# Two chains of attention maps in the second block, and joined small operations

## The chip, the cores and the metric

The kernel runs on one core of a Trainium2 chip. The metric is device microseconds (us) of one execution; lower is better. A core has a matrix engine (PE, with its weight loads shown apart as PEld), a vector engine (DVE), a scalar engine (ACT), a general engine (POOL) and a queue engine (SP) that issues most transfers. Each engine works through its own list of instructions in order, and waits at an instruction until what that instruction needs is there.

## The reference, cut to what matters

The program is two blocks of two layers on one sequence of 256 tokens and width 1024. The change lies in the second block alone, in its mixers; a layer there is:

```python
a = rms_norm_2(h, norm_attn[i])
u = a @ w_in[i]
(nsa_q, k_cmp, v_cmp, k_slc, v_slc, k_win, v_win, nsa_g, d_q, d_k, d_v,
 g_q, g_k, g_v, g_lr, g_og, r_q, r_f, r_i, r_og) = split_cols(u, IN_SPLITS_2)
o_a = nsa_attention(...)    # NSA: selected + window attention, a compressed branch, sigmoid gates
o_b = diff_attention(...)   # softmax(q0 k0) - lambda * softmax(q1 k1), times v, then an rms norm
o_c = gla_mixer(...)        # gated linear attention
o_d = hgrn2_mixer(...)      # gated linear attention with its own gate
h = h + jnp.concatenate([o_a, o_b, o_c, o_d], axis=-1) @ w_out[i]
...                         # a dense feed-forward (layer 0) or eight experts (layer 1)
```

and of the two mixers whose maps move:

```python
q = rms_norm_2(q, qk_gain[0])                       # NSA: also of k_slc and k_win
p = jax.nn.softmax(jnp.where(m, s, NEG), axis=-1)   # per head, causal
o = g[..., 0:1] * o_c + g[..., 1:2] * o_s + g[..., 2:3] * o_w
...
w = p[:, :, 0] - lam_full * p[:, :, 1]              # differential attention
o = rms_norm_2(einsum(w, v), sub_gain) * (1.0 - lam_init)
```

## The kernel before, in words

A projection is done in single-precision pieces: a 1 MB block of weights arrives by DMA (`raw`), ACT casts its high part (`whi`, line 142), DVE or POOL subtracts to get the low part (`wlo`, line 145), and PE does three products with the activations' high and low parts (lines 151 to 153). The 256 tokens are two tiles of 128, `tt` = 0 and 1.

`block2_mixers` runs once for each layer and does, in program order: the projection of the differential queries and keys, whose evacuation `ev_dqk` (lines 1216 to 1234) squares, sums, takes a power and scales; two projections for NSA and the differential values (`nsa`, `dv`); NSA's norms (squares `nsq` on POOL, sums `nr` on DVE, the power in `powm`, line 243, on POOL, the scaling `qn` on DVE, transposes `nqt` on PE); the compressed branch (`BT`, then the products `hp`); a projection for the linear attentions' values (tiles of 272 columns); the gate of gated linear attention (`glt`, `gp`, `gy`, with a logarithm on ACT); the channel projections (`pc`); seven *levels* (lines 1622 to 1684) that build the linear attentions' triangular matrices `AT`, each with the factors `E` and `Q` on DVE, an exponential on ACT, `Kt` on POOL, products `pg` and `ph` on PE and a masked copy on DVE; the *maps*; the projections of the output gates; norms, the transposes of `mix` (`ptr`, line 281) and the output projection.

A map is one softmax attention: `nsa_a`/`nsa_b` for a pair of heads of NSA, `diff_a`/`diff_b` for a pair of the differential mixer. The first half computes scores (`nl`, `dl`) and the softmax, the second transposes (`npt`, `dpt`), multiplies with the values (`npo`, `dpo`) and writes `mix`. There are eight per layer, and before the change all stand in one staggered chain: the second half of a map follows the first half of the next. Their PSUM tiles come from a ring of three (`pst`); the projections have another ring of three (`k.pmm`).

The order on each engine isn't written out by hand. The framework places instructions by a priority (the program order, or the number in `tc.cur_priority`) against its own estimate of when they can start. A tile of a ring waits until the tile that many turns earlier is no longer read; the working tiles `n2` of 128x512 numbers are a ring of six. The maps get the priority of an earlier place in the program:

```python
first = tc.cur_priority
...
last, tc.cur_priority = tc.cur_priority, first
staggered([(kind, tt, m) for tt in range(2) for m in range(2) for kind in (1, 0)], [map_a, map_b])
tc.cur_priority = last
```

Of the kernel before, what the change touches and what calls it, by code (L numbers as in the profile page):

```python
# [10 lines left out]
F32 = mybir.dt.float32  # L11
# [1114 lines left out]
def level_tiles(k):  # L1126

    k.qbg = k.lvl.tile([P, 2, 4, P], F32, tag="qbg", name="qbg")
    k.qbh = k.lvl.tile([P, 2, 2, 2, P], F32, tag="qbh", name="qbh")
    k.AT = k.lvl.tile([P, 2, 8, P], F32, tag="AT", name="AT")  # L1130
    k.nc.gpsimd.memset(k.qbg, 0.0)
    k.nc.gpsimd.memset(k.qbh, 0.0)
# [53 lines left out]
def block2_mixers(k, a, l, hl, pre):  # L1186
# [5 lines left out]
    with ExitStack() as es:  # L1192
# [8 lines left out]

        def w2(name):
            return k.lvl.tile([P, 512], F32, tag="w2", name=name, bufs=3)
# [12 lines left out]
        def ev_dqk(tt, ps):  # L1216
            sq = n2("dsq").rearrange("p (g d) -> p g d", d=32)
            nc.scalar.activation(sq, ps.rearrange("p (g d) -> p g d", d=32), AF.Square)
# [4 lines left out]
            dqk = n2("dqk").rearrange("p (g d) -> p g d", d=32)  # L1223
            nc.vector.tensor_tensor(dqk, ps.rearrange("p (g d) -> p g d", d=32),
                                    r[:, :, None].to_broadcast([P, 16, 32]), op=ALU.mult)
# [27 lines left out]
        proj_tok(k, [w[:, 512:652], w[:, 1164:1420]], 396, hl, ev_nd)  # L1253

# [34 lines left out]
        gates = one.tile([P, 2, 12], F32, name="ngate")  # L1289
        nc.scalar.activation(gates, nsa[:, :, 640:652], AF.Tanh, scale=0.5)  # L1290
        nc.vector.tensor_scalar(gates, gates, 0.5, 0.5, op0=ALU.mult, op1=ALU.add)
        g3 = gates.rearrange("p t (h g) -> p t h g", g=3)

# [116 lines left out]
        def softmax_map(lp, S, n, sc, name):  # L1410

            mx = sm.tile([P, n], F32, tag="mx", name="mx", bufs=8)
            nc.vector.tensor_reduce(mx, lp, axis=AX.X, op=ALU.max)
            nc.vector.tensor_scalar(mx, mx, -sc, None, op0=ALU.mult)
            su = sm.tile([P, n], F32, tag="su", name="su", bufs=12)
            pr = n2(name).rearrange("p (n s) -> p n s", n=n)
            for j in range(n):
                nc.scalar.activation(pr[:, j, :S], lp[:, j, :], AF.Exp, scale=sc, bias=mx[:, j : j + 1],
                                     accum_out=su[:, j : j + 1])
            return pr, su  # L1420

        def transposed(pr, tt, name):
            pt = pst(name).rearrange("p (n s t) -> p n s t", n=2, s=2)
            for n in range(2):
                for st in range(tt + 1):
                    nc.tensor.transpose(pt[:, n, st, :], pr[:, n, st * P : (st + 1) * P], k.ident)
            prT = n2(name + "T").rearrange("p (n s t) -> p n s t", n=2, s=2)
            nc.scalar.copy(prT[:, :, : tt + 1], pt[:, :, : tt + 1])
            return prT


        def nsa_a(kind, tt, m):
            S = P * (tt + 1)
            sl = slice(tt * P, (tt + 1) * P)
            lps = [pst(f"nl{j}").rearrange("p (n s) -> p n s", n=2) for j in range(2)]
            for n, kT in enumerate((kTs, kTw)):
                for j in range(2):
                    rows = slice(64 * j, 64 * j + 64)
                    nc.tensor.matmul(lps[j][:, n, :S], qT[rows, m, sl], kT[rows, :S], start=True, stop=False)
                for j in range(2):  # L1440
                    nc.tensor.matmul(lps[j][:, n, S - P : S], k.identb, k.ntrib, start=False, stop=True)
            r = []
            for j in range(2):
                pr, su = softmax_map(lps[j][:, :, :S], S, 2, 0.125, "npr")
                nc.vector.reciprocal(su, su)
                nc.vector.tensor_tensor(su, su, g3[:, tt, 2 * m + j, 1:3], op=ALU.mult)
                r.append((pr, su))
            return r

        def nsa_b(r, kind, tt, m):  # L1450
            for j in range(2):
                h = 2 * m + j
                pr, su = r[j]
                prT = transposed(pr, tt, "npt")
                po = pst("npo")[:, :128].rearrange("p (n d) -> p n d", n=2)
                for n in range(2):
                    vo = (448, 576)[n]
                    for st in range(tt + 1):
                        nc.tensor.matmul(po[:, n, :], prT[:, n, st, :], nsa[:, st, vo : vo + 64],
                                         start=st == 0, stop=st == tt)  # L1460
                o = mix[:, tt, O_NSA + 64 * h : O_NSA + 64 * h + 64]
                for n in range(2):
                    nc.vector.scalar_tensor_tensor(o, po[:, n, :], su[:, n : n + 1], o, op0=ALU.mult, op1=ALU.add)

        dsc = 32**-0.5

        def diff_a(kind, tt, par):

            S = P * (tt + 1)
            sl = slice(tt * P, (tt + 1) * P)  # L1470
            lps = [pst(f"dl{cc}").rearrange("p (n s) -> p n s", n=2) for cc in range(2)]
            for n in range(2):
                for cc in range(2):
                    rows = slice(32 * (2 * par + cc), 32 * (2 * par + cc) + 32)
                    nc.tensor.matmul(lps[cc][:, n, :S], dT[rows, n, sl], dT[rows, 2 + n, :S], start=True, stop=False)
                for cc in range(2):
                    nc.tensor.matmul(lps[cc][:, n, S - P : S], k.identb, k.ntrib, start=False, stop=True)
            e0, s0 = softmax_map(lps[0][:, :, :S], S, 2, dsc, "de0")
            e1, s1 = softmax_map(lps[1][:, :, :S], S, 2, dsc, "de1")
            nc.vector.reciprocal(s1, s1)  # L1480
            nc.vector.scalar_tensor_tensor(s1, s1, r2.nlam, s0, op0=ALU.mult, op1=ALU.mult)
            nc.vector.reciprocal(s0, s0)
            for n in range(2):
                nc.vector.scalar_tensor_tensor(e0[:, n, :S], e1[:, n, :S], s1[:, n : n + 1], e0[:, n, :S],
                                               op0=ALU.mult, op1=ALU.add)
            return e0, s0

        def diff_b(r, kind, tt, par):
            e0, s0 = r
            prT = transposed(e0, tt, "dpt")  # L1490
            po = pst("dpo")[:, :128].rearrange("p (n d) -> p n d", n=2)
            for n in range(2):
                h = 2 * n + par
                for st in range(tt + 1):
                    nc.tensor.matmul(po[:, n, :], prT[:, n, st, :], dv[:, st, 64 * h : 64 * h + 64],
                                     start=st == 0, stop=st == tt)
            for n in range(2):
                h = 2 * n + par
                nc.vector.tensor_scalar(mix[:, tt, O_DIFF + 64 * h : O_DIFF + 64 * h + 64], po[:, n, :],
                                        s0[:, n : n + 1], None, op0=ALU.mult)  # L1500
            if par == 1:

                mv = mix[:, tt, O_DIFF : O_DIFF + 256].rearrange("p (g d) -> p g d", d=64)
                sq = n2("dsq")[:, :256].rearrange("p (g d) -> p g d", d=64)
                nc.gpsimd.tensor_tensor(sq, mv, mv, op=ALU.mult)
                ss = sm.tile([P, 4], F32, tag="dss", name="dss")
                nc.vector.tensor_reduce(ss, sq, axis=AX.X, op=ALU.add)
                nc.vector.tensor_scalar(ss, ss, 1.0 / 64, EPS, op0=ALU.mult, op1=ALU.add)
                powm(k, ss, ss, -0.5)
                for g in range(4):  # L1510
                    o = mv[:, g]
                    nc.vector.scalar_tensor_tensor(o, o, ss[:, g : g + 1], r2.on[:, 0, :], op0=ALU.mult, op1=ALU.mult)

# [84 lines left out]
        for tt in range(2):  # L1598
            nc.gpsimd.tensor_tensor(k.AT[:, tt], k.ident[:, None].to_broadcast([P, 8, P]),
                                dg[:, tt, :, None].to_broadcast([P, 8, P]), op=ALU.mult)  # L1600
# [15 lines left out]
        for i, s in enumerate(LEVELS):  # L1616
# [27 lines left out]
            for tt in range(2):  # L1644
# [3 lines left out]
                for cb in range(2):  # L1648
                    nc.tensor.matmul(ph[:, tt, 2 * cb : 2 * cb + 2], Kt[:, 1 + cb, sl], Qh[:, cb, :, hs],
                                     start=True, stop=True)  # L1650
            for o, ps in ((0, pg), (4, ph)):
                if s >= 32:

                    for b in range(0, P, 2 * s):
# [503 lines left out]
```

## Time and profile before

| | us |
|---|---|
| median of three runs (lowest, highest) | 2427.41 (2426.46, 2427.61) |
| the profiled execution | 2425.61 |
| its span, first to last instruction | 2423.5 |
| PE busy | 2324.4 (96%) |
| DVE busy | 1873.6 (77%) |
| ACT busy | 1491.0 (62%) |
| POOL busy | 408.9 (17%) |

The mean granted TensorE clock is 0.986 of its full rate. On the time line the mixers of the second block's layer 0 lie at about 704 to 869 us and those of layer 1 at about 1174 to 1331 us; the eight experts follow and run to the end. In the rows below a time line gives start, duration, engine, line, operation, tiles (result <- inputs), shapes, count and, in brackets, how long the engine was idle before it and which instruction ended that. A row of windows gives a stretch, its length, and the busy time of each engine in it with the number of instructions.

### The profile page before, as it was taken

To read this page: it belongs to the slowest core of one execution; us is meant where nothing else is said; L and a number is where in the kernel's file an instruction comes from. 1 tells how busy PE (TensorE), PEld (TensorE's weight loads), DVE (VectorE), ACT (ScalarE), POOL (GpSimd) and SP (SyncE) were. 2 spreads that over 40 slices of the span, in tenths; PEclk is the share of its full clock that TensorE was granted. 3 is DMA by queue.
4 is the path that set the end of the run, shared out by engine and by line. 5 is a ranking of instruction groups with operands and counts; after the bars stand their busy time and mean duration, and the time that the engine had idled before them with its cause. 6 is when DMAs were issued, how large, how long until landed. Compare 5 with 4: busy or idle time off the path is not lost. (4 is left out here: it accounts for less than half of the span.)

```text
span 2423.5 us, 35194 instructions
## 1 busy us (share of the span) xinstructions
PE 2324.4 (96%) x13123; PEld 1949.1 (80%) x13123; DVE 1873.6 (77%) x2844; ACT 1491.0 (62%) x2333; POOL 408.9 (17%) x424
## 2 busy tenths in 40 slices
PE   8999999999999799999988999999999999999997
PEld 7898879888878689998776787887878777877775
DVE  5958576776766855556577799989998989898985
ACT  5455454455545754445466677777777777776763
POOL 3534114532142321111432100000000000000000
PEclk9999999999999899999999999999999999999998
DMA  8343254343346135555540999999999999999972
GB/s 249 105 139 123 88 170 158 122 140 108 128 153 199 40 131 180 186 189 182 164 157 25 351 364 345 371 331 364 361 349 330 354 345 346 346 350 348 345 256 88
DMA packets 288735, 550.07 MB, mean 227 GB/s; under 512 B 17414, under 2 KB 95020, under 8 KB 288300
## 3 DMA queue, kind: packets, MB, share of 16 engines
q1 hardware_dynamic: 287372, 546.67, 64.4%
q8 instruction: 105, 1.72, 0.3%
q0 software_dynamic: 144, 1.05, 0.1%
q14 instruction: 74, 0.61, 0.1%
q10 hardware_dynamic: 1040, 0.03, 0.0%
HBM read 545.61 MB, written 2.10 MB: 226 GB/s over the span
## 5 line engine op out<-in xcount | busy, mean ns | idle before, releaser
L145 DVE TENSOR_TENSOR wlo<-raw,whi 128x1024 fp32r<-128x1024 f32 x948 | 1143.2, 1236 | 267.8 <-ACT whi L142 260.5
L142 ACT CAST whi<-raw 128x1024 fp32r<-128x1024 f32 x984 | 1009.0, 1048 | 436.8 <-PE pt L153 92.1
L151 PE MATMUL pt<-whi,xh 128*128 128x512 f32 (+3 forms) x656 | 251.5, 395 | 14.6 <-DVE q L612 3.0
L152 PE MATMUL pt<-wlo,xh 128*128 128x512 f32 (+3 forms) x656 | 257.3, 393 | 2.9 <-DVE wlo L145 2.6
L153 PE MATMUL pt<-whi,xl 128*128 128x512 f32 (+3 forms) x656 | 253.0, 387 | 0.0
L243 POOL TENSOR_TENSOR nr<-nms,pwm 128x1 f32<-128x1 f32 x16 | 8.7, 547 | 1135.1 <-DVE nms L258 1135.0
L152 PE MATMUL mg<-wlo,xg 128*128 128x512 f32 x448 | 180.4, 403 | 3.3 <-DVE wlo L145 3.3
L152 PE MATMUL mu<-wlo,xg 128*128 128x512 f32 x448 | 179.1, 400 | 3.1 <-DVE wlo L145 3.1
L152 PE MATMUL ya<-wlo,hh 128*128 128x512 f32 x448 | 177.5, 397 | 0.1
L151 PE MATMUL mg<-whi,xg 128*128 128x512 f32 x448 | 177.2, 396 | 0.0
L153 PE MATMUL mg<-whi,xg 128*128 128x512 f32 x448 | 177.1, 395 | 0.0
L151 PE MATMUL mu<-whi,xg 128*128 128x512 f32 x448 | 177.0, 395 | 0.0
L153 PE MATMUL mu<-whi,xg 128*128 128x512 f32 x448 | 176.9, 395 | 0.0
L153 PE MATMUL ya<-whi,hl 128*128 128x512 f32 x448 | 175.8, 393 | 0.0
L151 PEld LDWEIGHTS pt<-whi,xh 128*128 128x128 f32 x656 | 124.9, 192 | 40.9 <-issue 8.7
L151 PE MATMUL pc<-xh,whi 128*128 128x256 f32 (+1 forms) x496 | 143.9, 290 | 5.8 <-DVE q L611 2.2
L152 PEld LDWEIGHTS pt<-wlo,xh 128*128 128x128 f32 x656 | 126.0, 192 | 28.4 <-DVE wlo L145 5.5
L151 PE MATMUL ya<-whi,hh 128*128 128x512 f32 x448 | 140.6, 394 | 5.6 <-ACT whi L142 5.6
L153 PEld LDWEIGHTS pt<-whi,xl 128*128 128x128 f32 x656 | 125.2, 191 | 22.8 <-DVE xl L284 1.1
L152 PE MATMUL pc<-xl,whi 128*128 128x256 f32 (+1 forms) x496 | 142.8, 288 | 0.0
L153 PE MATMUL pc<-xh,wlo 128*128 128x256 f32 (+1 forms) x496 | 142.7, 288 | 0.0
L151 PE MATMUL gu<-xh,whi 128*128 128x256 f32 x448 | 126.7, 283 | 0.0
(643 smaller groups left out, 4718.0 us busy)
## 6 DMA issues: line engine op xcount, KB each, us to landing
raw<-in_moe_w_gate SPq DMA_DIRECT2D x112, 1024.0 KB, 6.8
raw<-in_moe_w_up SPq DMA_DIRECT2D x112, 1024.0 KB, 6.7
raw<-in_moe_w_down SPq DMA_DIRECT2D x112, 1024.0 KB, 6.7
raw<-in_w_in SPq DMA_DIRECT2D x92, 1024.0 KB, 5.1
raw<-in_w_out SPq DMA_DIRECT2D x16, 1024.0 KB, 5.0
raw<-in_ffn_w_gate SPq DMA_DIRECT2D x14, 1024.0 KB, 5.1
raw<-in_ffn_w_up SPq DMA_DIRECT2D x14, 1024.0 KB, 5.3
raw<-in_ffn_w_down SPq DMA_DIRECT2D x14, 1024.0 KB, 5.6
```

The lines of the kernel that those rows point to most:

```text
L142: nc.scalar.copy(hi, raw_view)
L145: k.last_split = eng.tensor_sub(lo, raw_view, hi)
L151: nc.tensor.matmul(out, lh, rh, start=start, stop=False)
L152: nc.tensor.matmul(out, lh, rl, start=False, stop=False)
L153: return nc.tensor.matmul(out, ll, rh, start=False, stop=stop)
L243: return k.nc.gpsimd.tensor_tensor(out, in_, k.pw[e][:, :n], op=ALU.pow)
```

## The change

Four things are edited, all in `block2_mixers`. First, `ev_dqk` copies its PSUM tile to SBUF at once (ACT), and squares and scales from the copy. Second, the maps are issued in two chains. The differential maps of tile 0 are issued right after the projections of `nsa` and `dv`, ahead of NSA's norms, and NSA's maps of tile 0 at the place of the old chain, both from the old ring; the maps of tile 1 are issued after the last gate projection, from the projections' ring. Third, small operations are joined: one scaling of the maxima, one reciprocal and one gate product for two maps, one transposed tile and copy for two NSA heads of tile 0, one `npo` tile for two heads. `AT` gets another layout, so that two masked copies become one of double size. Fourth, the differential norm's last step, four DVE instructions of 64 columns, becomes one DVE product with the row norms and one POOL product with the gain.

```diff
         def ev_dqk(tt, ps):
+            dqk = n2("dqk").rearrange("p (g d) -> p g d", d=32)
+            nc.scalar.copy(dqk, ps.rearrange("p (g d) -> p g d", d=32))
             sq = n2("dsq").rearrange("p (g d) -> p g d", d=32)
-            nc.scalar.activation(sq, ps.rearrange("p (g d) -> p g d", d=32), AF.Square)
+            nc.scalar.activation(sq, dqk, AF.Square)
...
-            dqk = n2("dqk").rearrange("p (g d) -> p g d", d=32)
-            nc.vector.tensor_tensor(dqk, ps.rearrange("p (g d) -> p g d", d=32),
-                                    r[:, :, None].to_broadcast([P, 16, 32]), op=ALU.mult)
+            nc.vector.tensor_tensor(dqk, dqk, r[:, :, None].to_broadcast([P, 16, 32]), op=ALU.mult)
...
+        def softmax_maps(lps, S, sc, names):
+            mx = sm.tile([P, 2, 2], F32, tag="mx", name="mx", bufs=4)
+            for i, lp in enumerate(lps):
+                nc.vector.tensor_reduce(mx[:, i], lp[:, :, :S], axis=AX.X, op=ALU.max)
+            nc.vector.tensor_scalar(mx, mx, -sc, None, op0=ALU.mult)
...
+            if tt:
+                prTs = [transposed([pr], tt, "npt")[0] for pr, _ in r]
+            else:
+                prTs = transposed([pr for pr, _ in r], tt, "npt")
+            po = ring[0]("npo")[:, :256].rearrange("p (j n d) -> p j n d", j=2, n=2)
...
-                for g in range(4):
-                    o = mv[:, g]
-                    nc.vector.scalar_tensor_tensor(o, o, ss[:, g : g + 1], r2.on[:, 0, :], op0=ALU.mult, op1=ALU.mult)
+                nc.vector.tensor_tensor(mv, mv, ss[:, :, None].to_broadcast([P, 4, 64]), op=ALU.mult)
+                nc.gpsimd.tensor_tensor(mv, mv, r2.on[:, 0:1, :].to_broadcast([P, 4, 64]), op=ALU.mult)
+        def run(items, r):
+            ring[0] = r
+            staggered(items, [lambda kind, *it: (nsa_a, diff_a)[kind](kind, *it),
+                              lambda r, kind, *it: (nsa_b, diff_b)[kind](r, kind, *it)])
+        beside, done = ring
+        run([(1, 0, 0), (1, 0, 1)], beside)
...
-                for tt in range(2):
-                    nc.vector.copy_predicated(od4(k.AT[:, tt, o : o + 4, :]),
-                                              bs(k.lvm[s])[:, None].to_broadcast([P, 4, 64 // s, s]),
-                                              bs4(ps[:, tt]))
+                th = lambda ap: ap.rearrange("p t h i -> p (t h) i")
+                nc.vector.copy_predicated(od4(th(k.AT[:, o])),
+                                          bs(k.lvm[s])[:, None].to_broadcast([P, 8, 64 // s, s]), bs4(th(ps)))
...
-        staggered([(kind, tt, m) for tt in range(2) for m in range(2) for kind in (1, 0)], [map_a, map_b])
-        tc.cur_priority = last
+        run([(0, 0, 0), (0, 0, 1)], beside)
+        first, tc.cur_priority = tc.cur_priority, last
...
         proj_tok(k, w[:, 2716:3228], 512, hl, ev_rio)
+        last, tc.cur_priority = tc.cur_priority, first
+        run([(1, 1, 0), (0, 1, 0), (1, 1, 1), (0, 1, 1)], done)
+        tc.cur_priority = last
```

Two places of the resulting order matter. The first is POOL in layer 0, from the last product `dqk` of the differential keys to the clearing of the compressed branch's tiles `BT`. In the kernel before it is

```order
L145 TENSOR_TENSOR wlo<-raw,whi 128x792
L1228 TENSOR_TENSOR dqk<-dqk,bc_dqk_7484 128x256 x2
L1261 TENSOR_TENSOR nsq<-nsa 128x256
L1262 TENSOR_TENSOR nsq<-nsa 128x64
...
L145 TENSOR_TENSOR wlo<-raw,whi 128x1088
L1263 TENSOR_TENSOR nsq<-nsa 128x64 x2
L243 TENSOR_TENSOR nr<-nr,pwm 128x12
L1316 MEMSET BT 128x512 x2
```

and in the changed kernel, where `dsq` is the square of the differential mixer's output in `mix`, `dss` its norm and `mix<-mix,on` the product with its gain,

```order
L145 TENSOR_TENSOR wlo<-raw,whi 128x792
L145 TENSOR_TENSOR wlo<-raw,whi 128x1088
L1368 TENSOR_TENSOR dsq<-mix 128x256
L1390 TENSOR_TENSOR nsq<-nsa 128x256
L1391 TENSOR_TENSOR nsq<-nsa 128x64
L1392 TENSOR_TENSOR nsq<-nsa 128x64
...
L243 TENSOR_TENSOR dss<-dss,pwm 128x4
L243 TENSOR_TENSOR nr<-nr,pwm 128x12
L1374 TENSOR_TENSOR mix<-mix,on_7496 128x256
L1440 MEMSET BT 128x512 x2
```

So all six squares `nsq` now stand behind `dsq`, which reads the result of tile 0's differential maps. The same holds in layer 1.

The second is PE in layer 0 from the end of the values' projection (the tiles of 272 columns) to the first products `hp` of the compressed branch. Before it is

```order
L153 MATMUL pt_7910<-whi,xl 128x272
L1560 MATMUL glt<-cst,glt 16x128
L1283 MATMUL nqt<-cst,qn 128x128
...
L1566 MATMUL gp<-glr,wg_7980 128x256
L1283 MATMUL nqt<-cst,qn 128x128
L1475 MATMUL dl_8519<-dT 128x128
...
L1283 MATMUL nqt<-cst,qn 128x128 x3
L1329 MATMUL hp<-raw,BT 32x256 x8
```

and in the changed kernel

```order
L153 MATMUL pt_7994<-whi,xl 128x272
L1580 MATMUL glt<-cst,glt 16x128
L1358 MATMUL dpo<-dv,dptT 128x64 x2
...
L1286 MATMUL dpt<-cst,de_7873 128x128 x2
L1586 MATMUL gp<-glr,wg_8064 128x256
L1358 MATMUL dpo<-dv,dptT 128x64 x2
L1412 MATMUL nqt<-cst,qn 128x128 x6
L1453 MATMUL hp<-raw,BT 32x256 x8
```

The scores `dl` of tile 0 now stand earlier, among the projections, the last product `dpo` of tile 0's differential maps stands behind the gate's product `gp`, and the transposes `nqt` follow with no other work between.

## Rows read from the trace of the kernel before

**Rows 1.** Windows: stretch and length, busy time per engine, PE clock, DMA share, GB/s

```profile
704.00:740.40 36.40, 33.28 (x179) 28.31 (x178) 17.22 (x37) 13.43 (x24) 22.91 (x18) 0.91 0.61 195
740.40:753.45 13.05, 12.39 (x100) 6.37 (x97) 7.41 (x27) 7.68 (x17) 1.47 (x4) 0.87 0.55 166
753.45:789.50 36.05, 35.93 (x288) 32.97 (x285) 28.95 (x75) 23.01 (x60) 8.45 (x5) 1.00 0.52 175
789.50:833.60 44.10, 35.23 (x147) 26.26 (x145) 39.84 (x74) 29.07 (x73) 18.63 (x14) 0.77 0.16 54
833.60:868.90 35.30, 30.66 (x208) 25.91 (x208) 18.37 (x60) 19.96 (x57) 7.38 (x7) 0.95 0.00 1
...
1207.50:1219.10 11.60, 10.10 (x100) 5.67 (x100) 5.74 (x23) 6.95 (x17) 1.19 (x2) 1.00 0.82 253
1219.10:1258.40 39.30, 38.58 (x284) 35.14 (x284) 28.39 (x76) 25.13 (x62) 10.52 (x6) 0.96 0.46 156
1258.40:1296.70 38.30, 29.52 (x147) 22.27 (x147) 37.84 (x72) 27.72 (x70) 17.56 (x13) 0.91 0.19 62
1296.70:1331.50 34.80, 30.77 (x210) 25.98 (x209) 19.76 (x64) 20.03 (x58) 7.20 (x6) 0.95 0.00 1
```

**Rows 2.** Time line of PE, the projection behind the differential keys, both layers

```profile
713.77 0.77 PE L151 MATMUL pt<-whi,xh 128*128 128x512 f32 x1 [2.16 <-DVE dqk L1224]
714.34 0.63 PE L152 MATMUL pt<-wlo,xh 128*128 128x512 f32 x1
...
719.78 0.40 PE L151 MATMUL pt<-whi,xh 128*128 128x512 f32 x1
...
1182.35 0.47 PE L151 MATMUL pt<-whi,xh 128*128 128x512 f32 x1 [0.42 <-DVE dqk L1224]
```

**Rows 3.** Time line of PE, from the gate's product to the compressed branch, layer 0

```profile
741.82 0.69 PE L1566 MATMUL gp<-glr,wg 16*128 16x256 f32 x2 [0.34 <-ACT glr L1562]
...
742.70 0.48 PE L1475 MATMUL dl<-dT 32*128 32x128 f32 x2
...
744.19 1.07 PE L1329 MATMUL hp<-raw,BT 128*32 128x256 f32 x16
```

**Rows 4.** Time line of POOL, NSA's norms, layer 0

```profile
726.43 0.61 POOL L1261 TENSOR_TENSOR nsq<-nsa 128x256 f32<-128x256 f32 x1
727.00 0.28 POOL L1262 TENSOR_TENSOR nsq<-nsa 128x64 f32<-128x64 f32 x1
...
737.17 2.27 POOL L243 TENSOR_TENSOR nr<-nr,pwm 128x12 f32<-128x12 f32 x1 [1.08 <-DVE nr L1266]
739.38 0.99 POOL L1316 MEMSET BT<- 128x512 f32 x2
```

**Rows 5.** Time line of DVE, NSA's scaling and the compressed branch, layer 0

```profile
739.48 2.44 DVE L1277 SCALAR_TENSOR_TENSOR qn<-nsa,nr,bc_nsag 128x64 f32<-128x64 f32 x12 [2.38 <-POOL nr L243]
741.84 0.98 DVE L1321 TENSOR_TENSOR BT<-zt,pc 128x120 f32<-128x120 f32 x4
```

**Rows 6.** Time line of ACT, the logarithm of the gate, layer 0

```profile
745.23 1.28 ACT L1572 ACT_TABLE_LOAD   x1
```

**Rows 7.** Time line of DVE, the levels, layer 0

```profile
789.54 0.56 DVE L1624 TENSOR_TENSOR E<-gcat 128x384 f32<-128x384 f32 x1
...
794.07 2.25 DVE L1626 TENSOR_TENSOR E<-gcat 128x384 f32<-128x384 f32 x1
...
813.63 1.63 DVE L1512 SCALAR_TENSOR_TENSOR mix<-mix,dss,on 128x64 f32<-128x64 f32 x4
...
816.78 1.28 DVE L1659 COPY_PREDICATED AT<-lvm,pg 128x256 f32<-128x256 uint32 x2
```

**Rows 8.** Time line of POOL, the levels and the nearest product with a gain, layer 0

```profile
788.22 0.74 POOL L1723 TENSOR_TENSOR og<-og,on 128x256 f32<-128x256 f32 x1 [1.93 <-DVE og L1699]
...
793.76 4.31 POOL L1599 TENSOR_TENSOR AT<-cst,dg 128x1024 f32<-128x1024 f32 x2 [0.18 <-DVE dg L1597]
...
805.56 0.79 POOL L1505 TENSOR_TENSOR dsq<-mix 128x256 f32<-128x256 f32 x1 [0.95 <-DVE mix L1499]
```

## What I predicted, with its whole working

> **What bounds the kernel now.** I read the windows first, one for each stage of the two layers that the change touches [rows 1]. The reader is to see two kinds of stage. While the channel projections run, PE is busy for 35.93 of 36.05 us in layer 0 and 38.58 of 39.30 in layer 1: what leaves PE there shortens the stage, and nothing else does. In the stage of the levels DVE is busy for 39.84 of 44.10 us and 37.84 of 38.30 us, PE for less: there DVE sets the pace and PE waits. The last stage before the output projection has PE at 30.66 of 35.30 and 30.77 of 34.80 us. Then I read PE's time line where the change touches it, to see what ends its waits. Behind the differential keys PE waits 2.16 us in layer 0 and 0.42 us in layer 1 for DVE to release a PSUM tile [rows 2]. Between the values' projection and the channel projections almost nothing is lost: 0.66 us of 13.05 in layer 0, 1.50 of 11.60 in layer 1 [rows 1]. Last I read POOL, which is idle most of the time but carries NSA's norms: its powers end just before the DVE scaling that waited for them [rows 4, 5].
>
> I call the end of the values' projection V (740.40 us in layer 0, 1207.5 in layer 1) and the start of the channel projections P0 (753.45 and 1219.1).
>
> **The change part by part.** *The evacuation of the differential keys.* The copy to SBUF frees the tile without waiting for sum, power and scaling. The 2.16 us wait goes. Behind it PE ran at the lower clock (1.2 of 2.4 GHz): a product lasts 0.63 us at 714.34 and 0.40 at 719.78 [rows 2]. Twelve stand between; by 0.23 us they are 2.8 us, and as neighbours overlap I take 2.4. Layer 0 gains 2.16 + 2.4, about 4.6; layer 1 its 0.42 us and a little of the clock, 0.8. If another wait takes the place, the floor is nothing. The copy adds ACT work, which ACT's idle time hides, busy for 13.43 of the stage's 36.40 us [rows 1]; without that cover it would delay the keys' powers by the copy, and no matmul waits for these before the maps.
>
> *The differential maps of tile 0.* Their scores and transposes now stand among the projections ahead of V, where PE has no spare time, so V comes later by the matmuls that move. A pair of score products takes 0.48 us [rows 3] and there are eight pairs: 3.8 us; I leave the masks and transposes out, since part of them stays behind V. They are no longer in the channel projections and in the gap before: I take 3.1 us out of the stage in layer 0 and 4.3 in layer 1, where more of them stood. So the move alone is worth +0.7 and −0.5.
>
> *The norms behind them.* This is the term that decides. In the changed order POOL has the square `dsq` of tile 0's differential output ahead of all six `nsq`. That output is complete only after the last `dpo`, which stands behind `gp` on PE. Before, `gp` starts 1.4 us after V [rows 3] and takes 0.69; with the transposes' copy and DVE's write behind it, `mix` is there at about V+3. Then POOL: `dsq` 0.79 [rows 8], six squares 2 × (0.61 + 2 × 0.28) = 2.3 [rows 4], that is V+6. DVE's sum for NSA now stands behind the gate's subtraction, which waits for the logarithm with its table load of 1.28 us [rows 6]; V+8.5. The power takes 2.27 [rows 4]: V+10.8. The scaling takes 2.44 [rows 5]: V+13.2. The differential norm's POOL product (nearest row 0.74 [rows 8]) and the clearing of `BT`, 0.99 [rows 4], also stand ahead, the first beside the scaling; `BT`'s sum 0.98 [rows 5] brings the first `hp` to V+14. In the kernel before, `hp` starts at 744.19 and P0 comes 9.3 us later [rows 3]; less the scores that are gone from there, 8.5. So P0 = V+22.5, where before it was V+13.05 and V+11.6: +9.5 us in layer 0, +10.9 in layer 1. Nothing covers it, since PE has only `nqt` and `hp` behind `dpo`, and both need these norms. The bounds: nothing, if the maps end well before V so that POOL isn't held; and 2.4 us more per layer, the price of the lower clock behind a wait in the row above, if the wait costs the clock here too.
>
> *The stage of the levels and behind it.* Tile 0's differential maps and their norm leave DVE here: 1.63 us of products with the gain [rows 7], the sums and scalings around them, the joined maxima, reciprocals and gates, together about 4 us per layer by my count. The joined masked copy moves as many elements as before (two take 1.28 us [rows 7]), and I give it nothing. Since DVE is the pace, 4 us less of it are 4 us of time. In layer 0 the stage lasts 44.10 us at a clock of 0.77, in layer 1 38.30 at 0.91 for the same 147 matmuls [rows 1]; with the map work spread otherwise I expect some 4 of these 5.8 us back in layer 0. So −8 and −4. The bounds are nothing (DVE's list has as many `E` and `Q`, stretched beside POOL as before) and all the time in which PE is idle in the two last stages: 8.87 + 4.64 = 13.5 us in layer 0, 8.78 + 4.03 = 12.8 in layer 1 [rows 1].
>
> *A shared port.* A DVE product of 128x384 took 0.56 us alone and 2.25 while POOL built `AT` for 4.31 us [rows 7, 8]. The new POOL product with the gain falls beside the scaling on DVE. The Trainium skill (page "SBUF — State Buffer", section "Who interferes with whom") says that a DVE instruction with two inputs in SBUF contends with a GpSimd instruction that reads SBUF, through a shared port. The trace agrees with these 2.25 us. By it the evacuation's multiply, now from SBUF instead of PSUM, and the scaling would each be held for as long as the POOL product beside them; that would be up to 0.74 us more per layer, a sum of 4.7 us in place of 3.2.
>
> *Sum.* Layer 0: −4.6 + 0.7 + 9.5 − 8 = −2.4. Layer 1: −0.8 − 0.5 + 10.9 − 4 = +5.6. Together +3.2 us. Against the profiled execution's 2425.6 us (its span of 2423.5 and 2.1 around it) that is 2428.8; the median of the runs is 1.8 above that execution, so 2430.6, which I round to 2431. The experts, more than 1000 us, are not touched.
>
> **The rivals.** *The levels give back more (faster).* With tile 0's maps gone and tile 1's behind the gate projections, PE may have work for every wait of the levels, and the stages shorten by all their idle time: 13.5 + 12.8 = 26.3 in place of 12. Sum −11, 2416. For it: the low clock of 0.77 in layer 0, which is lost time on PE. Against it: DVE is full in this stage, and PE can't go faster than DVE releases the levels.
>
> *The norms are not held (faster).* If the maps end ahead of V, `dsq` waits for nothing and only half of the delay remains: +10 in place of 20, a sum of −7, 2420. For it: the scores stand well ahead of V. Against: the last `dpo` stands behind `gp` in PE's list, which can't start before V.
>
> *Nothing is given back (slower).* The wait of the norms is paid, and the stage of the levels stays as long as it is, because DVE's `E` and `Q` still stretch beside POOL and tile 1's maps, now in the projections' ring of three, hold up the gate projections by a tile that waits for a softmax. Then the 12 us are missing: +15, 2443. This decides from the point where the two stages give back less than 10 us over both layers, since the sum is then above 4.9. For it: ACT, at 29.07 and 27.72 us, has no less to do there. Against: the DVE work that leaves is real.
>
> *The maps don't really move*, because the framework's places come out the same in time: only the evacuation is left, −5.4, 2422.
>
> **How the numbers follow.** A difference below 0.2%, 4.9 us, can't be told from none here. Forecast 0.42, spread about 6 us around 2431; levels give back more 0.17; norms not held 0.12; nothing given back 0.24; maps don't move 0.05. Faster (below 2422.5): both faster cases, 0.27 after a little at their upper edge, and half of the last, 0.30. Within: somewhat more than half of the forecast, 0.25, and the rest of the small ones, 0.31. Slower (above 2432.3): 0.17 of the forecast and 0.22 of the last but one, 0.39. The range from 2415 to 2443 reaches to both ends' cases; the forecast's own is 2423 to 2439.
>
> **What would show it.** Right: on PE's time line a wait of some 9 us between the last `dpo` and the first `hp`, ended by DVE's `qn` or `BT`, with POOL's `dsq` starting about 3 us after V and `nsq` right behind; no wait on `dqk`; P0 22 us after V; the stage from P0 to the levels 3 to 4 us shorter; the levels and the last stage together 8 and 4 us shorter. Wrong: `nsq` before V; a P0 less than 17 us after V; or a stage of the levels as long as before with DVE no less busy.

## The result, and the profile after

The changed kernel takes 2443.84 us (median of four runs, 2442.65 to 2445.42) against 2427.51 before: ratio 1.0065, 95% interval 1.0052 to 1.0078, so 16.3 us slower. The profiled execution has a span of 2440.9 us, 17.4 more. That is outside the range I gave (2415 to 2443), by 0.8 us, and on the side of the rival "nothing is given back".

The windows of the kernel after, cut at the same four places of each layer as [rows 1] (V to P0, to the first factor `E`, the levels, the rest):

```profile
738.65:762.43 23.78, 14.02 (x111) 7.29 (x108) 12.39 (x41) 7.32 (x19) 9.65 (x16) 0.71 0.28 87
762.43:798.80 36.37, 36.37 (x282) 33.51 (x278) 27.18 (x56) 24.42 (x52) 9.87 (x6) 1.00 0.60 197
798.80:842.90 44.10, 34.30 (x145) 25.83 (x144) 37.18 (x61) 33.21 (x87) 18.16 (x13) 0.83 0.11 36
842.90:872.20 29.30, 28.32 (x178) 22.98 (x179) 14.40 (x38) 11.20 (x30) 5.60 (x5) 0.90 0.00 1
1214.10:1237.30 23.20, 13.27 (x112) 7.18 (x110) 11.58 (x40) 7.94 (x18) 9.62 (x16) 0.71 0.27 85
1237.30:1275.50 38.20, 38.06 (x289) 34.91 (x286) 26.38 (x60) 23.41 (x51) 11.08 (x7) 1.00 0.56 186
1275.50:1313.80 38.30, 32.16 (x117) 23.59 (x116) 34.60 (x53) 26.91 (x71) 13.47 (x11) 0.69 0.13 46
1313.80:1349.40 35.60, 32.79 (x203) 25.77 (x201) 15.82 (x42) 17.07 (x47) 6.89 (x6) 0.90 0.00 1
```

The first row of each layer holds the loss: 23.78 and 23.20 us where it was 13.05 and 11.60. Of the 10.7 and 11.6 us more, 9.1 and 8.4 are idle time of PE; it is busy for 1.6 and 3.2 us more, at a mean granted clock of 0.71 where it was 0.87 and 1.00 [rows 1]. PE's time line there shows one long wait in each layer, with the same work behind:

```profile
741.01 0.66 PE L1358 MATMUL dpo<-dv,dptT 128*128 128x64 f32 x4
750.76 0.87 PE L1412 MATMUL nqt<-cst,qn 128*128 128x128 f32 x2 [9.09 <-DVE qn L1406]
...
753.04 1.94 PE L1453 MATMUL hp<-raw,BT 128*32 128x256 f32 x16
...
1226.02 0.87 PE L1412 MATMUL nqt<-cst,qn 128*128 128x128 f32 x2 [9.13 <-DVE qn L1406]
```

The same sixteen products `hp` took 1.07 us before [rows 3] and take 1.94 behind the wait: the lower of the two clock levels. The kernel before ran at it in this stretch too, with no such wait ahead: thirty-two `hp` took 3.52 us at 750.00 us, and take 1.93 in the changed kernel, at 760.56 us. POOL's time line in layer 0 gives the chain that DVE's `qn` waited for:

```profile
727.29 2.60 POOL L145 TENSOR_TENSOR wlo<-raw,whi 128x1088 fp32r<-128x1088 f32 x1 [5.49 <-ACT whi L142]
742.33 0.66 POOL L1368 TENSOR_TENSOR dsq<-mix 128x256 f32<-128x256 f32 x1 [12.44 <-DVE mix L1362]
742.95 0.66 POOL L1390 TENSOR_TENSOR nsq<-nsa 128x256 f32<-128x256 f32 x1
...
747.37 2.37 POOL L243 TENSOR_TENSOR nr<-nr,pwm 128x12 f32<-128x12 f32 x1 [0.90 <-DVE nr L1395]
749.71 0.72 POOL L1374 TENSOR_TENSOR mix<-mix,on 128x256 f32<-128x256 f32 x1
```

POOL stands idle for 12.44 us with NSA's squares behind it, though the last of their inputs was in `nsa` before that idle time began (ACT's copy ended at 729.2 us); before, the first four of the six ran from 724.86 to 727.3 us (two of them in [rows 4]). DVE's sums of the squares, `nr`, start at 745.50 us, as the squares end, and stand behind the gate's subtraction, which waited for ACT's logarithm:

```profile
744.72 0.48 DVE L1594 TENSOR_TENSOR gy<-gy,gya 128x256 f32<-128x256 f32 x1 [1.26 <-ACT gya L1592]
```

Against the prediction's terms (us; before and after are cut at V, P0, the first `E` and the last transposes of `mix`, the start at the last transposes of the layer's input):

| | layer 0 predicted, measured | layer 1 predicted, measured |
|---|---|---|
| start to V | −0.8, −1.7 | +3.0, +2.2 |
| V to P0 | +9.5, +10.7 | +10.9, +11.5 |
| P0 to the levels | −3.1, +0.3 | −4.3, −1.1 |
| levels to the last transposes | −8, −4.9 | −4, +1.5 |
| sum | −2.4, +4.4 | +5.6, +14.1 |

What follows the last transposes of layer 1, the experts above all, takes 1.1 us less, which makes the 17.4.

### The profile page after: what moved, and what is told of

It is laid out like the page before. It is cut to its first block, busy times and chain, and to the rows that moved or that the text cites. A ratio compares the mean times of both kernels' runs of the same rounds, so it can differ in the third digit from the quotient of the medians.

```text
span 2440.9 us, 35118 instructions
## 1 busy us (share of the span) xinstructions
PE 2335.0 (96%) x13123; PEld 1953.9 (80%) x13123; DVE 1868.9 (77%) x2772; ACT 1493.2 (61%) x2333; POOL 412.1 (17%) x428
```

## The experiments

Every run was timed in five rounds beside the kernel before (2428 to 2429 us in each), with five to eleven executions. The last table gives all in one view.

**The parts apart.** `maps_back`, in the changed kernel:

```diff
-        run([(1, 0, 0), (1, 0, 1)], beside)
...
-        run([(0, 0, 0), (0, 0, 1)], beside)
+        run([(1, 0, 0), (0, 0, 0), (1, 0, 1), (0, 0, 1)], beside)
```

> The changed kernel with one thing undone: the differential maps of tile 0 stand again in one chain with NSA's of tile 0, at the priority of the old chain, so that they follow NSA's norms. All else of the change stays. Theory A (the norms behind the maps are the loss): the stretch from the end of the values' projection to the channel projections falls from 23.8 and 23.1 us to 12 to 14 us in both layers, POOL squares NSA's columns before that stretch begins, and the time is 2420 to 2427 us. Theory B (the maps of tile 1, behind the gate projections and in their ring, are the loss, and the wait in front only shifts work): the stretch shortens, but the levels and what follows lengthen by as much; 2437 us or more.

`dqk_alone` puts the new `ev_dqk` into the kernel before:

> The kernel before with the evacuation of the differential keys alone. Theory A, as the prediction had it: the wait of 2.16 us and the slow products behind it go in layer 0, 0.8 us in layer 1; 2421 to 2424 us. Theory B has nothing else to say of it. A rival of both: another wait takes its place (ACT, or the power on POOL), 2426 to 2428 us.

`joins_dqk` has all eight maps in one chain again:

```diff
-        run([(1, 0, 0), (1, 0, 1)], beside)
...
-        run([(0, 0, 0), (0, 0, 1)], beside)
+        run([(kind, tt, m) for tt in range(2) for m in range(2) for kind in (1, 0)], beside)
...
-        run([(1, 1, 0), (0, 1, 0), (1, 1, 1), (0, 1, 1)], done)
```

> The changed kernel without its two chains: all eight maps in one chain in the old ring at the old priority, with the joined small operations, the new layout of AT, the two-step differential norm and the new evacuation. Theory A: at least as fast as the evacuation alone, 2416 to 2424 us, since only DVE work is taken out. Rival: the joined tiles cost (two NSA heads wait for one another, one masked copy waits for both tiles' products); then it is slower than the evacuation alone, 2425 us or more.

Measured 2421.36, 2421.09 and 2414.42 us (ratios 0.9974, 0.9971 and 0.9944, each clear of 1 by its interval). So the early place of tile 0's differential maps costs the changed kernel 22.5 us: without it the front (the table's first column) is 31.3 us shorter and the back 6.4 longer. The evacuation gains 7.2 us, and the joins, with `AT`'s new layout and the two-step norm, another 6.7. For `maps_back` theory A holds and B falls; `dqk_alone` lies at the lower edge of A's range, `joins_dqk` 1.6 us below it.

**Why the early maps are dear.** `dnorm_late` issues tile 0's differential norm behind NSA's transposes (`if par == 1 and tt == 1: dnorm(tt)`, and `dnorm(0)` there):

> The changed kernel, with the maps of tile 0 ahead of NSA's norms as they are, but their differential norm (square, sum, power, two products) issued after NSA's transposes. POOL then has NSA's squares ahead of the differential square; they still need working tiles of the ring of six, whose turns the maps' exponentials hold until their transposes. Theory A: the squares start some 4 us earlier against the end of the values' projection, so each layer gains 3 to 5 us, and the time is 2434 to 2438 us; a part of the wait stays, from the ring and from the gate's chain on DVE. Theory B: no gain, 2442 to 2445 us.

`nsq_off_ring` changes the place of the squares alone:

```diff
-            sq = n2("nsq")[:, :384].rearrange("p (g d) -> p g d", g=6)
+            sq = mix[:, tt, O_GLA : O_GLA + 384].rearrange("p (g d) -> p g d", g=6)
```

> The changed kernel with one thing moved: NSA's squares are written to columns of mix that are written much later, not to working tiles of the ring of six. Nothing is issued in another place, and the differential norm stays ahead in the program. Without the ring POOL's list has all six squares and NSA's power ahead of the differential square. If the ring is what held the norms (theory A, made narrower: the squares need the turns that the maps' exponentials and transposes hold), the squares start 10 us or more ahead of the end of the values' projection, the stretch from there to the channel projections falls to 15 to 19 us, and the time is 2424 to 2432 us. If it is the place of the differential norm in the program, whatever the ring, it stays above 2438 us.

`off_ring_late` does both:

> NSA's squares off the ring and the differential norm after NSA's transposes, both together. If the ring alone decides: within 3 us of the run with the squares off the ring. If each has a part of its own: 3 to 8 us faster than that one, 2418 to 2426 us.

2427.36, 2427.97 and 2427.12 us: each takes some 16 us of the loss away, and both together no more. But they don't take the same 16 us. `nsq_off_ring` shortens the front by 13.3 us and the back by 3.9, as its theory A had it. `dnorm_late` did far more than I expected, and not for my reason: it shortens the front by only 4.8 us, and the back by 10.1, for which I have no cause. POOL's time line of `dnorm_late`, layer 0, shows the ring by itself:

```profile
735.88 0.61 POOL L1393 TENSOR_TENSOR nsq<-nsa 128x256 f32<-128x256 f32 x1 [4.65 <-DVE de L1347]
...
739.61 0.61 POOL L1393 TENSOR_TENSOR nsq<-nsa 128x256 f32<-128x256 f32 x1 [2.62 <-PE dpt L1286]
```

A square reads `nsa` and nothing of the maps, yet it waits for DVE's `de` and then PE's `dpt`: it needs the working tile that they release. The power behind these squares starts at 746.65 us all the same, after 5.93 us of waiting for DVE's `nr`, which still stands behind the gate's subtraction: with the squares earlier, DVE's order holds the norms. Off the ring the order on POOL turns round by itself, without a line issued elsewhere. POOL and PE of `nsq_off_ring`, layer 0:

```profile
734.21 2.27 POOL L243 TENSOR_TENSOR nr<-nr,pwm 128x12 f32<-128x12 f32 x1 [2.50 <-DVE nr L1395]
744.15 0.66 POOL L1368 TENSOR_TENSOR dsq<-mix 128x256 f32<-128x256 f32 x1 [7.67 <-DVE mix L1362]
```

```profile
745.14 0.87 PE L1412 MATMUL nqt<-cst,qn 128*128 128x128 f32 x2 [1.65 <-DVE qn L1406]
```

PE's wait falls from 9.09 to 1.65 us. `qn` and `BT` still take turns of the ring; `all_off_ring` moves them as well:

```diff
-            qn = n2("qn").rearrange("p (g d) -> p g d", d=64)
+            qn = (kcat, qcat)[tt][:, :2].rearrange("p a (g d) -> p (a g) d", d=64)
...
-            BT = [n2("BT").rearrange("p (m n) -> p m n", m=16) for _ in range(2)]
+            BT = [og[:, j].rearrange("p a (m n) -> p (a m) n", n=32) for j in range(2)]
```

> The changed kernel, its maps where the change put them, with all three consumers behind the maps taken off the ring of six: NSA's squares in columns of mix, its scaled queries and keys (qn) in kcat and qcat, the compressed branch's tiles BT in og, all of them tiles that are written later. If the ring alone made the early maps dear, the scaling starts ahead of the end of the values' projection again, the stretch to the channel projections is 13 us or less, and the time is 2416 to 2422 us, that of the run with the maps put back or below it. If the maps' own place on DVE and PE costs the rest, 2423 to 2428 us, as with the squares alone.

2422.14 us, a ratio of 0.9975 where `maps_back` has 0.9974. Its front is 99.1 us against 97.9: with no turn of the ring behind the maps, the early maps show no cost and no gain. The two runs differ in the ring as well as in the place of the maps, though, and taking the three tiles off the ring cost 8.7 us in the one chain (`off_ring_one_chain`, below); two chains with late maps and the tiles off the ring were not timed. So that the ring makes the front long is shown; that the early maps by themselves are worth nothing is not.

**The back.** `tile1_old_ring` is `maps_back` with `beside` in place of `done` for tile 1's maps; `after_old_ring` has that one edit in the changed kernel, `all_off_ring_old` in `all_off_ring`:

> The run maps_back (2421.4 us) with one more thing undone: the maps of tile 1, still issued after the gate projections, take their PSUM tiles from the old ring of three and no longer from the projections'. maps_back lay 7 us above the run with one chain. If the projections' ring costs that (a projection waits for a tile that a softmax holds): 2413 to 2418 us. If the later place in the program costs it, or the difference is one of runs: 2419 to 2424 us.

> The changed kernel, tile 1's maps in the old ring, still issued after the gate projections. If the projections' ring costs of itself: 2434 to 2439 us. If its effect depends on the order around it: anything from 2440 to 2448 us.

> The same, with the maps of tile 1 taking PSUM tiles from the old ring of three, still issued after the gate projections. If the projections' ring costs some 7 us here as it did with the maps put back: 2408 to 2415 us. If that cost came only with all tile 0 maps in the same chain: as all_off_ring, within 2 us.

2414.34 (−7.0 us), 2434.94 (−8.9) and 2426.52 us (+4.4). So the projections' ring cost 7 to 9 us in two settings and gained in a third, where the eleven executions of each run overlap in part. In layer 1 PE's longest wait in the back is 4.0 us in the kernel after, where a map's `dl` waits for `og`, a gate projection's evacuation, and 4.2 us in `after_old_ring`, where `dl` waits for another map's `mix`. The wait that can be seen there changes its name, not its size, so it doesn't explain the 9 us. From P0 to the last transposes of `mix`, layer 0 is 4.8 us shorter in `after_old_ring`, and PE idles there for 6.4 us in place of 10.8; layer 1 is 3.2 us shorter though PE idles for longer (10.5 us in place of 9.0), at a mean granted clock of 0.91 in place of 0.86.

`copies_single` is `joins_dqk` with the masked copies single again; `after_single`, `tile1_old_single` and `after_single_old` have that edit in the changed kernel, in `tile1_old_ring` and in `after_old_ring`:

```diff
-                th = lambda ap: ap.rearrange("p t h i -> p (t h) i")
-                nc.vector.copy_predicated(od4(th(k.AT[:, o])), ...
+                for tt in range(2):
+                    nc.vector.copy_predicated(od4(k.AT[:, o, tt]), ...
```

> The run joins_dqk with the masked copies single again: two of 256 columns for each joined one of 512, in the new layout of AT. The prediction gave the join nothing, since the elements are the same: 2413 to 2417 us. Rival, that each instruction carries a fixed price that the join saves twice per level: 2417 to 2420 us.

> The changed kernel with single masked copies. If the join costs of itself, as in the one chain: 2436 to 2441 us. If its 5 us there were an accident of one order: 2441 to 2447 us.

> The run tile1_old_ring (2414.3 us) with single masked copies. If the join costs of itself: 2407 to 2411 us. If not: 2412 to 2418 us.

> Both undone in the changed kernel. If both costs are of their own and add up: 2429 to 2434 us. If neither is: 2440 us or more.

2409.17 (−5.3 us), 2444.68 (+0.8), 2411.02 (−3.3) and 2439.88 us (+4.9). Only the first is clear of the scatter: its executions (2405.7 to 2411.4 us) all lie below those of `joins_dqk` (2413.1 to 2416.8), and its median below both ranges that I gave. The executions of the other three overlap with those of the run they are compared with, and those of `after_single_old` fall in two groups, 2435 to 2437 and 2443 to 2447 us, with nothing edited between them. So a cost of its own isn't shown for the join. The first of them gained in layer 1 alone, from the first `E` to the last transposes (64.2 us after 72.8), and nothing in layer 0 (75.4 after 75.3). In layer 1 it is PE's busy time that fell, not its waits: from P0 to the last transposes of `mix` 96.1 us after 105.3, at a mean granted clock of 0.95 after 0.90, and 8.5 us idle after 9.4.

`early_one_chain` keeps the early maps, with the squares off the ring and tile 1's maps in the old chain; `off_ring_one_chain` is `joins_dqk` with the three tiles off the ring:

> Squares off the ring, the differential maps of tile 0 ahead of NSA's norms, and all other maps in one chain in the old ring at the old priority. It asks whether the early maps pay once the norms aren't held. If they do, it is below the run with one chain and no early maps (2414.4 us): 2406 to 2413 us. If the early maps only put matmuls ahead of the channel projections that would have run beside them: 2414 to 2422 us.

> The run joins_dqk (one chain, no early maps, 2414.4 us) with the same three consumers off the ring of six. The compressed branch's products then come ahead of the values' projection's end. If the ring held nothing there before: 2413 to 2416 us. If the stretch between the values' projection and the channel projections shrinks, in which PE waited little: 2408 to 2413 us.

2415.45 and 2423.14 us. The first can't be told from `joins_dqk` (2414.4), so the early maps don't pay there. The second missed upwards by 7 us: `hp` runs ahead of V there, and the front is 10 us longer, not shorter.

All runs in two sums over both layers: the front, from the last transposes of the layer's input to P0, and the back, from P0 to the last transposes of `mix` (us). Front and back are those of the one profiled execution, the time is the median, and the two can differ by some us (`all_off_ring` was profiled at 2419.3, `after_single_old` at 2435.3):

| | front | back | time |
|---|---|---|---|
| before | 106.5 | 225.5 | 2427.5 |
| after | 129.2 | 221.4 | 2443.8 |
| after_single | 129.1 | 221.7 | 2444.7 |
| after_old_ring | 130.2 | 213.4 | 2434.9 |
| after_single_old | 129.3 | 215.7 | 2439.9 |
| dnorm_late | 124.4 | 211.3 | 2427.4 |
| nsq_off_ring | 115.9 | 217.5 | 2428.0 |
| off_ring_late | 115.8 | 217.2 | 2427.1 |
| early_one_chain | 117.3 | 207.6 | 2415.5 |
| all_off_ring | 99.1 | 224.3 | 2422.1 |
| all_off_ring_old | 99.7 | 227.7 | 2426.5 |
| off_ring_one_chain | 109.1 | 225.5 | 2423.1 |
| maps_back | 97.9 | 227.8 | 2421.4 |
| dqk_alone | 98.0 | 228.7 | 2421.1 |
| joins_dqk | 99.3 | 225.5 | 2414.4 |
| tile1_old_ring | 98.5 | 222.4 | 2414.3 |
| tile1_old_single | 98.0 | 218.7 | 2411.0 |
| copies_single | 98.4 | 216.1 | 2409.2 |

The lowest median is that of `copies_single`: one chain, the new evacuation, the joins without that of the masked copies; ratio 0.9921 (0.9907 to 0.9934).

## Why the prediction was wrong

*The norms behind the maps: right.* Place, cause on POOL and size: `dsq` at V+3.7 where I had V+3, `qn` at V+11.1 where I had V+10.8, P0 at V+23.8 where I had V+22.5. Of the 1.3 us over, 0.4 lie ahead of the first `hp` and 0.9 between it and P0, where the sixteen `hp` at the lower clock cost 0.9; I had kept that clock as a bound of 2.4 and left it out of the sum. DVE's sum stood behind the gate's subtraction, as I had it. What I didn't name is why POOL's list had `dsq` first: the ring of six. `nsq_off_ring` shows it.

*The evacuation: right in kind, too small.* PE waits for DVE's `dqk` no more, and alone it is worth 7.2 us where I had 5.4.

*The step that failed: "The stage of the levels and behind it", with the 7.4 us that I took out between P0 and the levels.* I forecast 19.4 us given back over the two layers; 4.2 came. Between P0 and the levels PE stayed as full as before, since the gate projections' products moved into the maps' place (and eight more `npo` of NSA's maps with them, in each layer). PE's work on `pt` in that stretch, first the kernel before and then after, both layers:

```profile
753.45:789.50 36.05, 7.04 (x51) 1.00 0.52 175
1219.10:1258.40 39.30, 8.71 (x58) 0.96 0.46 156
```

```profile
762.43:798.80 36.37, 9.66 (x61) 1.00 0.60 197
1237.30:1275.50 38.20, 10.21 (x66) 1.00 0.56 186
```

That work is then missing behind: layer 1's stage of the levels has 117 matmuls where it had 147, is as long (38.30 us), and shows a clock of 0.69 where it had 0.91 [rows 1]. DVE's work did leave (34.60 us busy after 37.84), and the stage didn't shorten; that DVE "sets the pace" there, and that 4 us less of it are 4 us of time, is the sentence that doesn't hold. From P0 to the last transposes of `mix` layer 1 shows what came in its place; first the kernel before, then after:

```profile
1219.10:1330.34 111.24, 98.39 (x635) 83.14 (x636) 85.81 (x208) 72.24 (x186) 35.27 (x25) 0.94 0.23 77
1237.29:1348.86 111.57, 102.54 (x603) 84.04 (x600) 76.81 (x152) 67.38 (x166) 31.45 (x24) 0.86 0.24 80
```

PE idles for 9.0 us where it idled for 12.9 and has 32 matmuls fewer, yet is busy for 4.2 us more, at a lower mean clock: behind the first `E` the 24 products `nl` take 10.07 us where they took 5.06. So time did come back as idle time, and went again at the lower clock level. The longest stretch at that level lies from 1289.1 to 1309.5 us and begins in the 4.0 us wait for `og`. I had a change of clock in layer 0 alone, as a gain; there the clock hardly moved from P0 on (0.91 after 0.90), and 4.9 of the 8 us came. Nor is it DVE's amount of work in the runs: edits that change that amount by next to nothing (the ring of tile 1's maps, the masked copies) moved the back by anything from 9.4 us down to 3.4 us up. The order in which the levels, the maps and the projections meet differs between these runs; that it decides how long the clock stays low is likely but not shown, and what in that order would do it stays open.

*The shared port.* By the sentence on the Trainium skill's page "SBUF — State Buffer" (section "Who interferes with whom") the new POOL product would hold the scaling by up to 0.74 us: `qn` took 2.89 us beside it, after 2.44 [rows 5], so the trace agrees, with 0.45. The first of its twelve instructions has all of that, 0.73 us where the others take 0.28, and ends within 0.1 us of the POOL product. DVE's line after is

```profile
749.77 2.89 DVE L1406 SCALAR_TENSOR_TENSOR qn<-nsa,nr,bc_nsag 128x64 f32<-128x64 f32 x12 [2.16 <-POOL nr L243]
```

*The chances.* The rival that came about, "nothing is given back", stood at 0.24 and its 2443 us is what was measured; the range ended there, 0.8 us short. That its number fits so well is luck: it still took out the 7.4 us between P0 and the levels, of which 0.8 came, and gave nothing back behind them, where 3.4 us came; and the ring of tile 1's maps, which it blamed, is worth 8.9 us of the changed kernel but 4.4 us the other way in `all_off_ring`.

## What to carry to other kernels

Before work is issued earlier, look through the rings that it takes tiles from: whatever is issued behind it and shares a ring inherits its waits, even where no data connect the two, and a framework that orders by readiness then puts it last. Work that leaves a stage of several engines isn't time that leaves it: count it as nothing until a wait is named that it ends, and compare the granted clock of the stage before idle time that went is called time won. When many edits come together, time each alone: here two were worth 14 us together and a third cost 22.

## What the runs showed of the hardware that I hadn't expected

The price of a wait on PE can go on behind it: sixteen `hp` products took 1.94 us after the wait of 9 us, at the lower of the two clock levels (1.2 of 2.4 GHz), and 1.07 before, without it. Such a wait isn't the only way there, as the thirty-two `hp` of the kernel before show. And waits of one length can come with different times at the lower level: in layer 1 the stretch that begins in the wait of 4.0 us lasts 20.4 us in the changed kernel, the one that begins in the wait of 4.2 us lasts 10.3 us in `after_old_ring`.
